# A scan's output store moved to two thirds of the next period, with a third output buffer (hybrid decoder trunk, one core)

## The chip, the core and the metric

The kernel runs on one core of a Trainium2 chip. Five engines work beside each other and meet through semaphores: PE (matrix products; PEld loads the stationary operand), DVE and ACT (elementwise work, also out of PSUM), POOL (elementwise work in SBUF) and SP, which here only issues transfers. Each engine takes its instructions in the order in which the program has them. The metric is device microseconds of one execution, the median of three runs.

## The reference, cut to what matters

Two layers run over 1024 tokens of width 1024: first a convolution and gating mixer, then RWKV-7 time mixing, each followed by a gated feed-forward network, with layer norms between. The change touches the recurrence of the second layer, with 16 heads of width 64:

```python
def step(state, inp):
    r_t, w_t, k_t, v_t, kk_t, a_t = inp
    sa = jnp.einsum('bhij,bhj->bhi', state, -kk_t)
    state = (state * w_t[:, :, None, :]
             + sa[..., None] * (kk_t * a_t)[:, :, None, :]
             + v_t[..., None] * k_t[:, :, None, :])
    return state, jnp.einsum('bhij,bhj->bhi', state, r_t)
_, y = lax.scan(step, state0, ...)
...
y = ((y - ym) * lax.rsqrt(yv + GN_EPS)).reshape(bsz, s, d) * ln_g + ln_b
y = y + bonus.reshape(bsz, s, d)
return ((y * g) @ w_out).astype(x.dtype)
```

## The kernel before, in words

The phases run one after another: `phase_a` (first mixer), `ffn`, `phase_c` (projections of the second mixer, spilled to DRAM), `phase_d` (the recurrence, "the scan"), `phase_e` (output projection) and `ffn` again. `phase_d` is a generator, which `phase_c` drives for its first steps and `phase_e` for the rest, with products of their own traced between its steps.

The scan cuts the 1024 positions into 16 chunks of 64 and the heads into two groups of 8. That makes 32 **units**, each a chunk of one group, in the order chunk by chunk. One turn of the loop at L1438 is a **period**. In period i several units are worked on at different stages, each a generator: `cumulate` (E in the order string; unit i+4), `decay` (D; unit i+3), `scores` (P; unit i+2), `inverse` (I; unit i+1) and `chain` (C; unit i). The string `ORDER` of 28 letters says which generator takes its next step. The order is that of tracing; a scheduler then sets each engine's own order from its model of durations and from the dependencies, so an operation may end up some periods ahead of where it was traced. A dependency made by `pace` only tells this scheduler to place an instruction behind the last product traced; on the chip nothing waits for it.

What matters here, with the lines of the profile:

- **Loads, all issued by SP**: `load` fetches the logarithmic decays SW and the keys KN (L1195, one tile `ld` for both), the keys K and KA (L1199, four transfers) and R (L1201). `load_v` fetches the values twice, into `UV` (L1211, a tile named `ra`) and into `V` (L1212, a tile named `R`), two transfers each. The names of tiles in a profile are those of the big tile from which a ring of small buffers was cut, so `R` stands for many things and the line tells them apart.
- **`cumulate`**: DVE's running sum over SW (L1218), then L1221; ACT's exponentials of it (L1224, L1226, L1228).
- **`decay`**: ACT L1238 and L1239, DVE L1243, L1246, L1247, POOL L1249.
- **`inverse`**: five levels of small products (pX, pQ), each with an ACT copy (L1304) and two DVE copies (L1313, L1317).
- **`chain`**: products with the state, ACT copies (L1345, L1351, L1356, L1366), the state's update (DVE L1375, POOL L1376), then statistics of the output on DVE (L1386, L1387), ACT L1389, and a run of POOL operations on the output y: L1391, L1395, L1396, L1397, L1400 and L1407, where y is done. POOL's L1399 prepares `bo`, the bonus that L1400 adds; it reads `V`, and there are three buffers of `V` and two of `bo`.
- **`store`** (L1418): two transfers of y to DRAM (L1422), traced at the start of the next period, ahead of that period's loads.

So one instruction stream on SP carries 13 transfers for each unit: 2 stores and 11 loads. `phase_e` reads y back in rows of 128 tokens (L174 from `scr_y`), loads the weights `w_o` (L174) through three `wraw` buffers, and splits them on ACT (L189) and DVE (L190); some of that is traced into the last periods of the scan.

Of the kernel before, what the change touches and what calls it, by code (L numbers as in the profile page):

```python
# [72 lines left out]
AHEAD = 4  # L73
INV = 1

ORDER = "ICIPCEIPDICPIECDICPICICPDICI"
SCAN_EARLY = 32


# [77 lines left out]
def small(c, shape, name, tag, bufs=4):  # L157
    return c.pool.tile(shape, F32, name=name, tag=tag, bufs=bufs)


def bank(c, which, name, shape=None, dtype=F32):
    return c.psum.tile(shape or [P, 512], dtype, name=name, tag="ps" + which,
                       bufs=dict(a=NB_A, b=NB_B, c=NB_C)[which])
# [39 lines left out]
def pace(c, ins):  # L203

    return after(c, ins, c.last_mm)


def after(c, ins, dep):

    c.tc.add_manual_dep(ins.ins, dep.ins.name, mybir.DependencyInfo(  # L210
        mybir.DependencyClass.NoSync, mybir.DependencyReason.SCHED_ONLY), reason="pace")
    return ins
# [836 lines left out]
def level_view(ap, m, second):  # L1049

    v = ap.rearrange("p h (b e m) -> p h b e m", e=2, m=m)
    return v[:, :, :, 1 if second else 0, :]
# [71 lines left out]
def phase_d(c, scr, scrv, scry, l_g2):  # L1124
# [10 lines left out]
    nc, tc, sc = c.nc, c.tc, c.scan  # L1135
    NG = NH // 2 // HP
# [5 lines left out]
    half = [slice(0, 64), slice(64, 128)]  # L1142
# [3 lines left out]
    def rings(plan, n, dtype=F32):  # L1146
        pool, at = Ring(c, plan[0][0], n, sum(k for _, k in plan), dtype).bufs, 0
        for name, k in plan:
            r = Ring.__new__(Ring)
            r.bufs, r.i = pool[at:at + k], 0  # L1150
            at += k
            R1[name] = r
    rings([("ra", INV + 3), ("bk", 2), ("bktm", NA), ("UV", INV + 3), ("AT", 2 * NA)], 2 * W)
    rings([("R", 3), ("cl", 2), ("Em", 2), ("rk", 2), ("S", 2 * NG), ("dS", 2), ("u1", 2), ("y", 2),
           ("V", 3), ("gg", 2), ("bo", 2)], W)
    rings([("E", 4)], HP * (CH + 2))
    rings([("TT", 2)], HP * P, F32R)
# [4 lines left out]
    for i, t_ in enumerate(R1["AT"].bufs):  # L1162
        e = 1 - i % 2
# [5 lines left out]
    S = [None] * NG  # L1169
# [9 lines left out]
    def mm(*a, **k):  # L1179
        keep(nc.tensor.matmul(*a, **k))  # L1180

    def tr(*a):
        keep(nc.tensor.transpose(*a))

    def load(n, ch, g):
        u = Ctx()
        u.n, u.ch, u.g = n, ch, g
        ks = slice(g * HP, (g + 1) * HP)
        at = slice(ch % 2 * CH, ch % 2 * CH + CH)
        src = lambda nm, r=slice(0, P): scr[nm][ch // 2, r, ks, at]  # L1190
        u.ld = {}
        t_ = tmp(c, "ld")
        for e, nm in enumerate(("SW", "KN")):
            u.ld[nm] = A4(t_[:, e * W:(e + 1) * W])
            nc.sync.dma_start(u.ld[nm], src(nm))  # L1195
        u.xk = tmp(c, "ld").rearrange("p (k x t) -> p k x t", k=HP, x=2)
        for e in range(2):
            for x, nm in ((e, "K"), (1 - e, "KA")):
                nc.sync.dma_start(u.xk[half[e], :, x, :], src(nm, half[e]))  # L1199
        u.ld["R"] = A4(R1["R"]())  # L1200
        nc.sync.dma_start(u.ld["R"], src("R"))  # L1201
        us[n] = u

    def load_v(u):

        src = scrv[u.ch * CH:(u.ch + 1) * CH, u.g * 2 * W:(u.g + 1) * 2 * W].rearrange(
            "t (k e j) -> t e k j", k=HP, e=2)
        u.UV = R1["UV"]().rearrange("p (e k j) -> p e k j", e=2, k=HP)
        u.V = A4(R1["V"]())
        for e in range(2):  # L1210
            nc.sync.dma_start(u.UV[half[e], e], src[:, e])  # L1211
            nc.sync.dma_start(u.V[half[e]], src[:, e])  # L1212
# [21 lines left out]
    def decay(u):  # L1234

        ld = u.ld
        E, Em = u.clx, A4(R1["Em"]())
        nc.scalar.activation(Em, E[:, :, 1:CH + 1], AF.Exp, scale=CDEC)  # L1238
        nc.scalar.activation(E[:, :, 1:CH + 1], E[:, :, 1:CH + 1], AF.Exp, scale=-CDEC)  # L1239
        u.ra = A4(R1["ra"]())  # L1240
        u.bk, u.rk = A4(R1["bk"]()), A4(R1["rk"]())
        yield
        nc.vector.tensor_tensor(u.bk.rearrange("p k (x t) -> p k x t", x=2), u.xk,  # L1243
                                Em.unsqueeze(2).to_broadcast([P, HP, 2, CH]), op=ALU.mult)
        yield
        nc.vector.tensor_tensor(u.ra[:, :, 0:CH], ld["R"], E[:, :, 1:CH + 1], op=ALU.mult)  # L1246
        nc.vector.tensor_tensor(u.ra[:, :, CH:], ld["KN"], E[:, :, 0:CH], op=ALU.mult)  # L1247
        for e in range(2):
            nc.gpsimd.tensor_tensor(u.rk[half[e]], ld["R"][half[e]], u.xk[half[e], :, e, :], op=ALU.mult)  # L1249
        yield  # L1250

    def scores(u):
        u.AT = [A4(R1["AT"]()) for _ in range(2)]
        u.lt = A4(R1["lt"]())

        ps = [bank(c, "c", "pA", [P, HP, P]) for _ in range(2)]
        for k, e in PAIRS:
            mm(ps[e][:, k, :], u.bk[half[e], k, :], u.ra[half[e], k, :], start=True, stop=True)
            if (k, e) == (HP // 2 - 1, 1):
                yield  # L1260
        for e in range(2):
            nc.vector.copy_predicated(u.AT[e], sc.mA.rearrange("p k x t -> p k (x t)"), ps[e])
            o = half[1 - e]
            nc.scalar.copy(u.lt[o, :, o], u.AT[e][o, :, CH:])
        yield

        pb = bank(c, "c", "pb")
        for k, e in PAIRS:
            mm(pb[half[e], k:k + 1], u.rk[half[e], k, :], c.colr("r_k", u.g * HP + k, 1)[half[e]],
               start=True, stop=True)  # L1270
        u.bon = small(c, [P, HP], "bon", "bon", NA)
        nc.vector.tensor_copy(u.bon, pb[:, 0:HP])
        yield

        p = bank(c, "c", "ptm", [P, HP, P])
        for k in range(HP):
            tr(p[:, k, :], u.bk[:, k, :], c.ident)
        u.bktm = A4(R1["bktm"]())
        nc.scalar.copy(u.bktm, p)
        u.Tm, u.Tt = A4(R1["Tm"]()), A4(R1["Tt"]())  # L1280
        idb = sc.ident16.unsqueeze(1).to_broadcast([P, HP, P])
        nc.scalar.copy(u.Tm, idb)
        nc.scalar.copy(u.Tt, idb)
        yield
        u.L = A4(R1["L"]())
        p16 = bank(c, "b", "pL", [P, HP, P], F16)
        for k in range(HP):
            tr(p16[:, k, :], u.lt[:, k, :], sc.ident16)
        nc.scalar.copy(u.L, p16)
        nc.vector.copy_predicated(level_view(u.Tt, 1, True), sc.mTT[1].unsqueeze(3), level_view(u.lt, 1, True))  # L1290
        nc.vector.copy_predicated(level_view(u.Tm, 1, False), sc.mT[1].unsqueeze(3), level_view(u.L, 1, False))
        yield
# [118 lines left out]
    seq = [(ch, g) for ch in range(T // CH) for g in range(NG)]  # L1411
    us = {}

    def through(gen):
        for _ in gen:
            pass

    def store(u):  # L1418
        dst = scry[u.ch * CH:(u.ch + 1) * CH, u.g * 2 * W:(u.g + 1) * 2 * W].rearrange(
            "t (k e j) -> t e k j", k=HP, e=2)  # L1420
        for e in range(2):
            nc.sync.dma_start(dst[:, e], u.y[half[e]])  # L1422

    def by_half(name):

# [11 lines left out]
    through(decay(us[0]))  # L1437
    for i in range(-INV - 1, len(seq)):  # L1438
        gens = {}
        if i > 0:  # L1440
            store(us[i - 1])
        if i + AHEAD + 1 < len(seq):
            load(i + AHEAD + 1, *seq[i + AHEAD + 1])
        if 0 <= i + INV + 1 < len(seq):
            load_v(us[i + INV + 1])
        if i + AHEAD < len(seq):
            gens["E"] = cumulate(us[i + AHEAD])
        if i + INV + 2 < len(seq):
            gens["D"] = decay(us[i + INV + 2])
        if i >= 0:  # L1450
            gens["C"] = chain(us[i], us.get(i + NG))
        if 0 <= i + INV < len(seq):
            gens["I"] = inverse(us[i + INV])
        if i + INV + 1 < len(seq):
            gens["P"] = scores(us[i + INV + 1])
        if i == 0:
            g2 = c.pool.tile([P, 1024], F32, name="g2", tag="w", bufs=N_W)
            nc.sync.dma_start(g2, l_g2)
            g2 = g2.rearrange("p (g k e j) -> p g e k j", g=NG, k=HP, e=2)
            lg, lb = by_half("rln_g"), by_half("rln_b")  # L1460
        for s in ORDER:
            if s in gens:
                fresh[0] = True
                next(gens[s], None)
                if s in "CIP":
                    yield
        for gen in gens.values():
            assert next(gen, "end") == "end"
    store(us[len(seq) - 1])

def phase_e(c, scry, xres, w_o, scan, res):
# [52 lines left out]
    def through(gen):  # L1527
        for _ in gen:
            pass
    total = 32 * sum(ORDER.count(s) for s in "CIP") - SCAN_EARLY  # L1530
    rows_ = [big(c, "g_row"), c.pool.tile([P, 1024], F32, name="b_row", tag="w", bufs=N_W)]
# [112 lines left out]
```

## Time and profile before

| | us |
|---|---|
| median of three runs (2683.39, 2683.41, 2695.26) | 2683.41 |
| the profiled execution | 2686.94 |
| its span, first to last instruction | 2685.1 |
| SP's wait for L1407 or L1399 at L1422, 1420 to 1862 us | 172.5 |
| DVE's wait for SW at L1218, same stretch | 24.3 |

The page gives busy time by engine and in 40 slices. The views used below are the windows (busy time of each engine in a stretch, and the granted clock), the waits (who waited for whom, in total) and the timelines of single engines, where a bracket behind a row is the idle time before it and what ended it. A wait for several semaphores is put down to the one that came last.

### The profile page before, as it was taken

To read this page: it belongs to the slowest core of one execution; us is meant where nothing else is said; L and a number is where in the kernel's file an instruction comes from. 1 tells how busy PE (TensorE), PEld (TensorE's weight loads), DVE (VectorE), ACT (ScalarE), POOL (GpSimd) and SP (SyncE) were. 2 spreads that over 40 slices of the span, in tenths; PEclk is the share of its full clock that TensorE was granted. 3 is DMA by queue.
4 is the path that set the end of the run, shared out by engine and by line. 5 is a ranking of instruction groups with operands and counts; after the bars stand their busy time and mean duration, and the time that the engine had idled before them with its cause. 6 is when DMAs were issued, how large, how long until landed. Compare 5 with 4: busy or idle time off the path is not lost. (4 is left out here: it accounts for less than half of the span.)

```text
span 2685.1 us, 41451 instructions
## 1 busy us (share of the span) xinstructions
PE 2533.1 (94%) x16064; PEld 2018.1 (75%) x16064; DVE 1672.4 (62%) x2981; ACT 1135.9 (42%) x2192; POOL 505.3 (19%) x526
## 2 busy tenths in 40 slices
PE   8999989999989999999998888888899999998998
PEld 7677867888868787777777767776778888876776
DVE  7675596666645427777846767675387666644435
ACT  3116542333324217777746666574252333323320
POOL 0012250000041000010214555456200000023003
PEclk9999999999999998999998889799899999998999
DMA  3403322222245322555764343323122222235531
GB/s 143 124 25 114 107 85 88 86 77 81 79 160 199 135 99 95 168 153 177 203 165 101 92 95 88 69 48 131 67 102 102 79 79 86 79 130 183 177 106 63
DMA packets 258181, 297.89 MB, mean 111 GB/s; under 512 B 149952, under 2 KB 191040, under 8 KB 257984
## 3 DMA queue, kind: packets, MB, share of 16 engines
q1 hardware_dynamic: 256832, 293.14, 34.4%
q8 instruction: 126, 2.06, 0.3%
q10 hardware_dynamic: 1152, 2.10, 0.2%
q14 instruction: 71, 0.58, 0.1%
HBM read 221.66 MB, written 69.21 MB: 108 GB/s over the span
## 5 line engine op out<-in xcount | busy, mean ns | idle before, releaser
L641 PE MATMUL py<-xch,wb 128*128 128x512 f32 x1056 | 356.6, 400 | 4.4 <-DVE u L690 2.4
L229 PE MATMUL pd<-wb,hh 128*128 128x512 f32 x704 | 282.2, 401 | 21.9 <-ACT wb L197 14.2
L197 ACT CAST wb<-wraw 128x512 fp32r<-128x512 f32 x220 | 135.2, 619 | 376.8 <-PE py L641 173.9
L231 PE MATMUL pd<-wb,hl 128*128 128x512 f32 x704 | 281.9, 400 | 6.9 <-DVE hl L200 6.9
L230 PE MATMUL pd<-wb,hh 128*128 128x512 f32 x704 | 281.4, 400 | 1.5 <-DVE wb L200 1.5
L200 DVE TENSOR_TENSOR wb<-wraw,wb 128x512 fp32r<-128x512 f32 x220 | 161.0, 735 | 145.1 <-ACT wb L197 143.0
L641 PEld LDWEIGHTS py<-xch,wb 128*128 128x128 f32 x1056 | 200.3, 190 | 62.8 <-DVE u L690 15.7
L641 PE MATMUL pz<-xch,wb 128*128 128x512 f32 x704 | 233.4, 393 | 4.5 <-ACT xch L197 4.5
L641 PE MATMUL px<-xch,wb 128*128 128x512 f32 x704 | 233.9, 395 | 3.2 <-ACT p L652 3.2
L352 POOL TENSOR_TENSOR acc<-acc,g_row 128x1024 f32<-128x1024 f32 x24 | 62.4, 2605 | 845.3 <-DMA acc<-res 824.0
L197 ACT CAST wb<-sums 128x512 fp32r<-128x512 f32 x176 | 108.6, 621 | 257.1 <-PE pz L641 144.3
L641 PE MATMUL py<-xcl,wb 128*128 128x512 f32 x528 | 209.4, 397 | 1.6 <-DVE xcl L200 1.6
L200 DVE TENSOR_TENSOR wb<-sums,wb 128x512 fp32r<-128x512 f32 x176 | 123.2, 703 | 102.3 <-ACT wb L197 101.5
L200 DVE TENSOR_TENSOR hl<-wraw,hh 128x1024 fp32r<-128x1024 f32 x76 | 107.1, 1411 | 115.8 <-ACT hh L197 115.8
L229 PEld LDWEIGHTS pd<-wb,hh 128*128 128x128 f32 x704 | 135.7, 193 | 55.7 <-ACT wb L197 15.5
L231 PEld LDWEIGHTS pd<-wb,hl 128*128 128x128 f32 x704 | 135.0, 192 | 38.2 <-DVE hl L200 7.8
L1180 PEld LDWEIGHTS <-lt 128*128 128x128 f16 x1792 | 88.5, 103 | 97.1 <-issue 71.3
L230 PEld LDWEIGHTS pd<-wb,hh 128*128 128x128 f32 x704 | 135.2, 192 | 33.4 <-DVE wb L200 2.7
L641 PEld LDWEIGHTS pz<-xch,wb 128*128 128x128 f32 x704 | 132.5, 189 | 34.5 <-ACT xch L197 5.3
L641 PEld LDWEIGHTS px<-xch,wb 128*128 128x128 f32 x704 | 131.9, 188 | 34.9 <-ACT p L652 5.5
L269 POOL TENSOR_TENSOR rstd<-ve,mhalf 128x1 f32<-128x1 f32 x48 | 37.9, 792 | 627.0 <-DVE ve L267 590.9
L1180 PE MATMUL pX<-lt 128*128 128x64 f16 x1280 | 92.3, 201 | 63.1 <-DVE lt L1313 33.4
(311 smaller groups left out, 5779.4 us busy)
## 6 DMA issues: line engine op xcount, KB each, us to landing
wraw<-in_f_in_dram SPq DMA_DIRECT2D x96, 512.0 KB, 3.6
wraw<-scr_h SPq DMA_DIRECT2D x76, 512.0 KB, 3.9
scr_h<-hf SPq DMA_DIRECT2D x44, 512.0 KB, 2.6
wraw<-in_f_out_dram SPq DMA_DIRECT2D x88, 256.0 KB, 3.0
res<-acc SPq DMA_DIRECT2D x16, 512.0 KB, 2.6
acc<-res SPq DMA_DIRECT2D x16, 512.0 KB, 6.7
wraw<-in_w_r_dram SPq DMA_DIRECT2D x16, 512.0 KB, 3.8
wraw<-in_w_k_dram SPq DMA_DIRECT2D x16, 512.0 KB, 4.2
```

Of the source, the lines that this page charges most:

```text
L197: nc.scalar.copy(hi, src)
L200: return (eng or nc.vector).tensor_tensor(lo, src, f(hi), op=ALU.subtract)
L229: nc.tensor.matmul(ps, ls(ah), rs(bh), start=start, stop=False)
L230: nc.tensor.matmul(ps, ls(ah), rs(bl), start=False, stop=False)
L231: c.last_mm = nc.tensor.matmul(ps, ls(al), rs(bh), start=False, stop=stop)
L269: c.last_pow = nc.gpsimd.tensor_tensor(r, ve, c.mhalf[:, 0:1], op=ALU.pow)
L352: c.nc.gpsimd.tensor_tensor(x, x, rows[0], op=ALU.mult)
L641: c.last_mm = nc.tensor.matmul(ps, a_[:, k * P:(k + 1) * P], b_[:, k % 2, :], start=start and k == i == 0, stop=False, skip_group_check=True)
L1180: keep(nc.tensor.matmul(*a, **k))
```

## The change

`store` becomes a generator with one step, its two transfers carry a `pace`, and a letter Y in `ORDER`, the 21st of now 29 letters, says where that step is taken. It still stores the unit of the period before. The ring of y buffers grows from two to three; the rings of that plan take 27 in place of 26 quarter tiles, and seven big tiles hold 28.

```diff
-ORDER = "ICIPCEIPDICPIECDICPICICPDICI"
+ORDER = "ICIPCEIPDICPIECDICPIYCICPDICI"
...
-    rings([("R", 3), ("cl", 2), ("Em", 2), ("rk", 2), ("S", 2 * NG), ("dS", 2), ("u1", 2), ("y", 2),
+    rings([("R", 3), ("cl", 2), ("Em", 2), ("rk", 2), ("S", 2 * NG), ("dS", 2), ("u1", 2), ("y", 3),
...
         for e in range(2):
-            nc.sync.dma_start(dst[:, e], u.y[half[e]])
+            pace(c, nc.sync.dma_start(dst[:, e], u.y[half[e]]))
+        yield
...
-        if i > 0:
-            store(us[i - 1])
         if i + AHEAD + 1 < len(seq):
             load(i + AHEAD + 1, *seq[i + AHEAD + 1])
...
             gens["P"] = scores(us[i + INV + 1])
+        if i > 0:
+            gens["Y"] = store(us[i - 1])
...
-    store(us[len(seq) - 1])
+    through(store(us[len(seq) - 1]))
```

The scheduler's order changes on SP, ACT, DVE and POOL and not on PE. Three places follow. A number in a name is a buffer, and a bracket names the semaphores that an instruction waits for: `Pool_49` counts POOL's instructions, `DMAHWn_49` earlier transfers.

**SP, in the middle of the scan.** Before, the store of unit 14 stood ahead of `V` of unit 19 (L1212) and of SW of unit 23:

```order
L1422 DMA scr_y_81<-R_10298 64x4x64 [waits DMAHW5_49,Pool_49]
L1422 DMA scr_y_81<-R_10298 64x4x64 [waits DMAHW6_49]
L1212 DMA R_10299<-scr_v_80 64x4x64 [waits DMAHW7_49,Pool_49]
L1212 DMA R_10299<-scr_v_80 64x4x64 [waits DMAHW0_49]
L1195 DMA ld_13762<-scr_SW_79 128x4x64 [waits DMAHW1_49,DVE_49]
```

In some periods the next unit's SW stood ahead of the store, as here SW of unit 24 and the store of unit 15:

```order
L1195 DMA ld_14008<-scr_SW_79 128x4x64 [waits DMAHW2_49,DVE_49]
L1422 DMA scr_y_81<-R_10298 64x4x64 [waits DMAHW3_49,Pool_49]
L1422 DMA scr_y_81<-R_10298 64x4x64 [waits DMAHW4_49]
L1212 DMA R_10299<-scr_v_80 64x4x64 [waits DMAHW5_49,Pool_49]
L1212 DMA R_10299<-scr_v_80 64x4x64 [waits DMAHW6_49]
```

Now every period has this order, here with `V` of unit 19, SW of unit 23 and the store of unit 14:

```order
L1212 DMA R_10299<-scr_v_80 64x4x64 [waits DMAHW6_49,Pool_49]
L1212 DMA R_10299<-scr_v_80 64x4x64 [waits DMAHW7_49]
L1195 DMA ld_13760<-scr_SW_79 128x4x64 [waits DMAHW0_49,DVE_49]
L1195 DMA ld_13760<-scr_KN_77 128x4x64 [waits DMAHW1_49]
L1201 DMA R_10294<-scr_R_75 128x4x64 [waits DMAHW2_49,DVE_49,Pool_49]
L1422 DMA scr_y_81<-R_10298 64x4x64 [waits DMAHW3_49]
L1422 DMA scr_y_81<-R_10298 64x4x64 [waits DMAHW4_49]
```

The store has moved behind SW, KN and (mostly) R, and has lost its wait for POOL; the first of the two `V` loads keeps one, and now stands ahead of SW in every period. In both programs the counts say that `V` of unit n waits for L1399 of unit n-3, which stands on POOL directly behind L1407 of unit n-5, the output that the store of unit n-5 takes.

**DVE, around L1218 of unit 20** (the profile names this operation TENSOR_TENSOR_SCAN). Before:

```order
L1313 COPY_PREDICATED lt<-mk_1_3128,pX 128x32x8
L1317 COPY_PREDICATED lt<-mk_0_3122,pQ 128x32x8
L1243 TENSOR_TENSOR ra<-ld,R 128x512
L1218 SCALAR_TENSOR_TENSOR R<-rst,ld 128x256
L1375 TENSOR_TENSOR R<-pS,R 128x256
```

Now:

```order
L1313 COPY_PREDICATED lt<-mk_1_3128,pX 128x32x8
L1317 COPY_PREDICATED lt<-mk_0_3122,pQ 128x32x8
L1218 SCALAR_TENSOR_TENSOR R<-rst,ld 128x256
L1243 TENSOR_TENSOR ra<-ld,R 128x512
L1375 TENSOR_TENSOR R<-pS,R 128x256
```

In 15 of the 22 units from 10 to 31 L1218 now stands ahead of L1243 and L1375, and in the other 7 between the two. ACT's L1238, which needs L1243, stands behind L1224 in the 15 units, and ahead of it in the 7. Before, L1218 stood at varying places: where SW was ahead of the store it stood up to six rows earlier, ahead of L1246.

**SP, at the end of the scan.** Before, a `w_o` load stood behind the store of unit 29:

```order
L174 DMA wraw_18532<-in_w_o_dram 128x1024 [waits DMAHW4_49,DMAHW1_49,DVE_49]
L1422 DMA scr_y_81<-R_10298 64x4x64 [waits DMAHW5_49,Pool_49]
L1422 DMA scr_y_81<-R_10298 64x4x64 [waits DMAHW6_49]
L174 DMA wraw_18538<-in_w_o_dram 128x1024 [waits DMAHW7_49,DMAHW3_49,DVE_49]
L174 DMA wraw_18544<-scr_y_81 128x1024 [waits DMAHW4_49,DMAHW0_49,DVE_49]
L1494 DMA acc_18548<-xres_74 128x1024
L174 DMA wraw_18594<-scr_y_81 128x1024 [waits DMAHW7_49,DMAHW2_49,DVE_49]
```

Now:

```order
L174 DMA wraw_18532<-in_w_o_dram 128x1024 [waits DMAHW4_49,DMAHW1_49,DVE_49]
L174 DMA wraw_18538<-in_w_o_dram 128x1024 [waits DMAHW5_49,DMAHW3_49,DVE_49]
L174 DMA wraw_18544<-scr_y_81 128x1024 [waits DMAHW6_49,DMAHW4_49,DVE_49]
L1495 DMA acc_18548<-xres_74 128x1024 [waits DMAHW7_49]
L174 DMA wraw_18594<-scr_y_81 128x1024 [waits DMAHW5_49,DMAHW0_49,DVE_49]
L1422 DMA scr_y_81<-R_10298 64x4x64 [waits Pool_49]
L1422 DMA scr_y_81<-R_10298 64x4x64 [waits DMAHW2_49]
```

The last `w_o` load of the scan, two rows of y, and a load of the residual have moved ahead of that store. The `w_o` load's own wait for DVE is for the L190 that frees its `wraw` buffer, the second of the five at the end of the scan.

## Rows read from the trace of the kernel before

**Rows 1.** Page: the span.
```profile
span 2685.1 us, 41451 instructions
```
**Rows 2.** Windows: stretch, length, busy by engine, clock, DMA share, GB/s.
```profile
1440.41:1757.55 317.14, 267.85 (x4494) 229.45 (x4493) 221.82 (x643) 204.04 (x599) 170.84 (x223) 0.85 0.37 87
1650.33:1662.44 12.11, 10.80 (x208) 9.19 (x204) 9.62 (x29) 9.09 (x27) 7.37 (x10) 1.00 0.33 73
1739.89:1754.82 14.93, 14.27 (x209) 12.43 (x206) 10.04 (x29) 9.59 (x29) 5.48 (x8) 0.66 0.29 64
```
**Rows 3.** Waits, 1420 to 1862: total us, times, longest.
```profile
DVE R L1218 <- DMA ld<-scr_SW: 24.3, 12, 3.8
...
SPq L1422 <- POOL R L1399: 145.2, 28, 11.1
SPq L1422 <- POOL R L1407: 27.3, 3, 13.0
```
**Rows 4.** Timeline of POOL: unit 11's y, then unit 12's.
```profile
1583.08 0.73 POOL L1407 TENSOR_TENSOR R<-R 128x256 f32<-128x256 f32 x1
1583.77 0.61 POOL L1399 TENSOR_TENSOR R<-R,bon 128x256 f32<-128x256 f32 x1
...
1597.97 0.72 POOL L1407 TENSOR_TENSOR R<-R 128x256 f32<-128x256 f32 x1
```
**Rows 5.** Timeline of SP's issues in the same stretch.
```profile
1583.84 1.25 SPq L1422 DMA_DIRECT2D scr_y<-R  x2
1585.19 1.25 SPq L1212 DMA_DIRECT2D R<-scr_v  x2
1586.54 0.55 SPq L1195 DMA_DIRECT2D ld<-scr_SW  x1
```
**Rows 6.** Timeline of DVE in the same stretch.
```profile
1586.13 0.69 DVE L1243 TENSOR_TENSOR ra<-ld,R 128x512 f32<-128x512 f32 x1
1589.72 0.69 DVE L1218 TENSOR_TENSOR_SCAN R<-rst,ld 128x256 f32<-128x256 f32 x1 [2.90 <-DMA ld<-scr_SW]
```
**Rows 7.** Timeline of PE in the same stretch.
```profile
1591.12 0.28 PE L1180 MATMUL pX<-lt 128*128 128x64 f16 x4 [2.57 <-DVE lt L1313]
```
**Rows 8.** Timeline of SP, then of DVE, around the store of unit 16.
```profile
1648.37 0.36 SPq L1195 DMA_DIRECT2D ld<-scr_SW  x1
1652.74 1.25 SPq L1422 DMA_DIRECT2D scr_y<-R  x2
...
1653.48 1.21 DVE L1218 TENSOR_TENSOR_SCAN R<-rst,ld 128x256 f32<-128x256 f32 x1
```
**Rows 9.** DMA view, 1440 to 1757: KB each, median us to landing.
```profile
ld<-scr_SW SPq DMA_DIRECT2D x22, 128.0 KB, 2.5
```
**Rows 10.** Timeline of SP, then of DVE: the slowest SW that was waited for.
```profile
1628.03 0.55 SPq L1195 DMA_DIRECT2D ld<-scr_SW  x1
...
1632.63 0.69 DVE L1218 TENSOR_TENSOR_SCAN R<-rst,ld 128x256 f32<-128x256 f32 x1 [1.42 <-DMA ld<-scr_SW]
```
**Rows 11.** A window, and the gap of PE ahead of it.
```profile
1733.00:1750.50 17.50, 17.10 (x210) 14.65 (x211) 11.05 (x37) 9.76 (x30) 7.53 (x11) 0.51 0.29 65
...
1732.94 0.28 PE L1180 MATMUL pX<-lt 128*128 128x64 f16 x4 [3.22 <-DVE lt L1313]
```
**Rows 12.** Timelines of SP, DVE, ACT and PE at the scan's end, and its window.
```profile
1837.84 1.25 SPq L1422 DMA_DIRECT2D scr_y<-R  x2
1839.19 0.54 SPq L174 DMA_DIRECT2D wraw<-in_w_o_dram  x1
...
1829.62 1.22 DVE L190 TENSOR_TENSOR wlo<-wraw,whi 128x1024 fp32r<-128x1024 f32 x1 [2.02 <-ACT whi L189]
...
1843.33 1.04 ACT L189 CAST whi<-wraw 128x1024 fp32r<-128x1024 f32 x1 [9.68 <-DMA wraw<-in_w_o_dram]
...
1844.97 0.37 PE L1180 MATMUL pX<-lt 128*128 128x64 f16 x4 [6.06 <-ACT lt L1304]
...
1842.00:1849.50 7.50, 4.53 (x24) 3.57 (x24) 1.89 (x3) 2.40 (x6) 3.48 (x2) 0.54 0.75 279
```

## The prediction

> **What bounds the kernel now.** The profiled execution took 2686.94 us, its span 2685.1 [rows 1], 3.5 above the median of 2683.41; the sum below is made against 2686.94 and 3.5 are taken off at the end. I read the windows of the scan first. From the store of unit 1 to that of unit 23 are 317.14 us, 22 periods of 14.42 on average. A period without a stall takes 12.11 us at clock 1.00 and 14.93 at a granted clock of 0.66, with PE busy for 10.80 and 14.27 of it [rows 2]. So PE and the chain behind it set a period of about 12 us at 2.4 GHz, and the missing 2.3 us are stalls and stretches at 1.2 GHz. The mean clock of 0.85 says that about 30% of the time is at the lower level (1 - 0.3 x 0.5).
>
> The waits come next. SP waits 172.5 us at the store, 145.2 and 27.3 in two rows, and DVE waits 24.3 us for SW in 12 units [rows 3]. SP's large number costs nothing by itself; what costs is what stands behind it. The timelines of unit 11 show how: POOL ends y (L1407) at 1583.81 [rows 4]; SP, which had waited for that, issues the store at 1583.84, `V` at 1585.19 and SW only at 1586.54 [rows 5]; DVE is through with L1243 at 1586.82, and L1218 starts at 1589.72, having waited 2.90 [rows 6]; PE has a gap of 2.57 [rows 7]. Where SW stood ahead of the store there is none of this: SW issued at 1648.37, the store at 1652.74, and L1218 starts at 1653.48 without a wait [rows 8].
>
> **The scan: the store.** The change takes the store's two issues from ahead of `V` and SW to behind SW and KN. Taken alone, that frees SW from POOL's L1407. But `V` keeps its wait for POOL, which is for L1399, the instruction behind the same L1407, and the order now has `V` ahead of SW in every period. So I expect the wait to move from the store to `V`: SP stands at L1212 where it stood at L1422, and SW, KN and R stand behind it as before. What is won is the store's own time in that queue, 1.35 us (1583.84 to 1585.19, [rows 5]); what is lost is L1399, which ends 0.57 after L1407 (1583.77 + 0.61 against 1583.81, [rows 4]). The net gain is 0.78 us in a unit that stalls today. Against it stand the 10 units of 22 that don't stall today, in which SW would now stand behind the wait too.
>
> **The period that follows.** The stalled unit is a loop from one L1407 to the next. (1) L1407 to `V`: 0.57 + 0.03 for the issue = 0.60. (2) `V`'s pair to SW: 1.35 [rows 5]. (3) SW's issue to L1218: the median landing is 2.5 [rows 9]; unit 11 had 3.18 (1589.72 - 1586.54, [rows 5, 6]); the slowest had 4.60 [rows 10]. I take 2.8, between the median and unit 11, because the store's transfers are no longer just ahead of it; the ends are 2.5 and 4.6. (4) L1218 to the next end of L1407: 8.97 (1589.72 to 1598.69, [rows 4, 6]). These make 13.72. In 15 of the 22 units L1243, and with it ACT's L1238, now stand behind the waiting L1218, where in unit 11 they were done before it. That adds nothing if the chain has slack there, and L1243's 0.69 [rows 6] and a hand-over of about 0.2 (my estimate) if it has none. I take 0.85, near the upper end, since L1375, which carries the chain on, stands behind L1243 on DVE; the ends are 0 and 0.9. So 7 units of 13.72 and 15 of 14.57 make a mean of 14.30, at 2.4 GHz.
>
> **The clock.** A stall in every period makes a gap of PE in every period. After the gap of 3.22 that ended at 1732.94 the clock was 0.51 for 17.5 us [rows 11]. A low period of the old kernel took 14.93 [rows 2]; the loop hides part of that, as (1) to (3) don't depend on PE, and I give a low period 15.2 in place of 14.30. Today 30% of the time is low with 12 stalls; with a stall in each period I take 40%. That is 0.4 x 0.9 = 0.36, and a period of 14.66 against 14.42: 22 x 0.24 = **+5.3**. The ends of (3) and (4) move it widely: landing at the median is -0.3 a period, 22 x 0.3 = 6.6 lower; unit 11's 3.18 in place of 2.8 is 8.4 higher; L1243 at no cost is 15 x 0.85 = 12.8 lower. The slowest landing in every period would be 22 x 1.8 = 40 higher, which one row out of 22 doesn't make likely.
>
> A rule on step (3): the page DMA: Bandwidth & Descriptors of the Trainium skill, section Anatomy of one DMA — SWDGE (gpsimd) path, gives a transfer a fixed 2.0 us and its bytes at 436 GB/s; for 128 KB that is 2.3 us, an estimate from that page. The trace disagrees upward, with 2.5 as the median and 3.18 and 4.60 where DVE waited [rows 5, 6, 9, 10], and the page states it for POOL's path while these are issued by SP. By the page the sum would be 0.5 x 22 = 11 us lower.
>
> **The end of the scan.** Here the change does take a transfer out from behind the wait. The store of unit 29 went out at 1837.84 and the `w_o` load behind it at 1839.19, though that load's buffer was free when L190 ended at 1830.84; ACT got it at 1843.33 after a wait of 9.68, and PE had a gap of 6.06, followed by 7.5 us at clock 0.54 [rows 12]. Now the load stands ahead of that store, issues at about 1831 and lands by 1835 (the same 4.14 us), some 1.4 us after ACT falls idle (1843.33 - 9.68 = 1833.65). The gap goes, -6.06, and some of the slow clock, where PE was busy for 4.53 of 7.50: half of that at the lower level would be given back, about 2. With 1 us for what is late next (DVE's L190 behind ACT's L189) I take **-7**; the ends are -4 (the load still meets `V` loads ahead of it) and -9.
>
> **Edits at nothing.** The `pace` is no wait on the chip. The third y buffer takes the 27th of 28 quarter tiles, so no other ring shrinks; a y is stored about half a period later than before, and the third buffer gives it a whole period more. The loads of y for `phase_e` stand behind later stores, but those of the last units stay behind the same L1407. PE's order doesn't change. If the store's 2 x 0.6 us on SP were to stand where SW is due, the cost would be 1.35 a period, but it stands behind SW.
>
> **Sum.** 2686.94 + 5.3 - 7 = 2685.2; less 3.5 makes a forecast of **2682**.
>
> **Rival A, faster: no wait takes the store's place.** If POOL has done L1399 by the time SP comes to `V`, SW lands before DVE needs it in all units, as in the units with SW ahead of the store [rows 8]. The period would be 12.11 with a few at the low clock, 12.3: 22 x (14.42 - 12.3) = 47 less, and 7 at the end: 2683 - 54 = 2629. Half of that, where `V` is late in every other unit, gives 2656. Against it: in the timeline L1399 ends 0.57 us behind the very instruction for which SP waits today [rows 4], and SP has no more to do ahead of it than before. Chance 0.17.
>
> **Rival B, slower: the clock stays low through the scan.** Place: PE's gap in each period behind L1218. If each gap of 2 us or so is followed by a low stretch as long as a period, as at 1733 to 1750.5 [rows 11], all periods are low ones, of 14.93 and what the loop doesn't hide, 15.4 by my estimate: 22 x 0.98 = 21.6 more, less 7: 2698. It decides, against my bound of 13.4, from a period of 14.42 + (13.4 + 7)/22 = 15.35, or from SW landing 0.7 later than I took it. For it: nearly every unit gets a gap; against it: in the loop at low clock PE fills its own gap, since a PE that needs 14.27 of 14.93 [rows 2] has none. The page TensorE: Matmul & The Clock Gate of the Trainium skill, section A second HAM failure mode: psum-queue depth-cycling, says that short idling of PE between groups, often repeated, makes the clock swing between its two levels. By that rule this rival comes true; the trace agrees as far as one gap of 3.22 and the 0.51 behind it go. Chance 0.26.
>
> **The forecast's own case** is that the change doesn't do what it says: the store moves and the wait stays. Chance 0.57, with a range of its own of 2670 to 2697.
>
> **How the numbers follow.** Within 0.5% (13.4 us, about what a measurement of this kernel can tell from no change) lies 2670 to 2697. The range that leaves out 2 in 10 cuts off rival A beyond its mildest third and the upper third of rival B, where slow landings add to a low clock: 2664 to 2704.
>
> **What would show it.** Right: SP's wait for L1399 stands at L1212 and none at L1422; L1218 waits for SW in about 22 units, 35 to 50 us in all; the mean period is 14.2 to 15.2; ACT's wait of 9.68 and PE's gap of 6.06 at the end are gone. Wrong towards A: L1218 waits for SW seldom, and a period is below 13. Wrong towards B: the clock over the same 22 periods is below 0.75. Wrong in the tail: the `w_o` load still lands after 1840.

## The result, and the profile after

The changed kernel is slower: 2703.60 us against 2684.85 (medians of 11 runs each); the ratio of the means is 1.0058, with an interval of 1.0041 to 1.0075. The forecast was 2682, which could not be told from no change; the time lies in the stated range, but as a loss, on the side of rival B. The profiled execution took 2705.01, its span is 18.2 us longer than that of [rows 1]:

```profile
span 2703.3 us, 41451 instructions
```

Where the 18.2 went follows from the ends of L1407 of units 1 and 23, 22 periods apart (in the kernel before at 1440.38 and 1757.52, [rows 2] to within 0.03). The 22 periods took 341.51 in place of 317.14: **+24.4**. From there to the end are 919.9 us (2703.3 - 1783.41) in place of 927.6: **-7.7**. Ahead of unit 1 is +1.5.

The windows of the kernel after; the columns are those of [rows 2]. The first row is the 22 periods, the next two are the periods of units 16 and 17, and the last two are stretches cut where the clock changes:

```profile
1441.90:1783.41 341.51, 296.22 (x4486) 254.08 (x4485) 216.05 (x642) 204.03 (x599) 169.22 (x223) 0.74 0.36 80
1660.10:1674.38 14.28, 11.53 (x160) 9.64 (x161) 7.66 (x27) 8.41 (x25) 7.38 (x12) 0.74 0.34 76
1674.38:1691.02 16.64, 15.84 (x252) 13.92 (x251) 11.24 (x33) 9.80 (x31) 7.25 (x12) 0.71 0.31 66
...
1667.00:1684.50 17.50, 16.70 (x206) 14.34 (x204) 10.18 (x36) 9.94 (x30) 7.23 (x10) 0.51 0.30 66
1684.50:1697.50 13.00, 10.41 (x204) 9.01 (x200) 8.43 (x23) 8.01 (x25) 7.17 (x10) 1.00 0.36 78
```

Two kinds of period take turns here, 14.28 and 16.64 (the next two are 14.12 and 16.63). This holds for the last ten of the 22; the twelve ahead of them have no such order and take 13.5 to 18.9. Over the pair the clock is at 1.2 GHz for 17.5 us and at 2.4 for the rest. The mean period is 15.52 and the mean clock 0.74, where it was 14.42 and 0.85.

The waits of DVE, SP and ACT, 1420 to 1880 us (total, times, longest), which answer to [rows 3]:

```profile
DVE R L1218 <- DMA ld<-scr_SW: 29.3, 15, 3.3
...
ACT whi L189 <- DMA wraw<-in_w_o_dram: 3.8, 2, 2.4
...
SPq L1212 <- POOL R L1399: 134.8, 27, 7.4
...
SPq L1422 <- POOL R L1399: 17.7, 2, 11.1
```

The wait has moved from the store (145.2) to `V` (134.8), as forecast; the waits left at the store are those at the end of the scan. The timelines of POOL, SP, DVE and PE over that pair of periods answer to [rows 4 to 7]:

```profile
1659.37 0.73 POOL L1407 TENSOR_TENSOR R<-R 128x256 f32<-128x256 f32 x1
1673.65 0.73 POOL L1407 TENSOR_TENSOR R<-R 128x256 f32<-128x256 f32 x1
1690.29 0.73 POOL L1407 TENSOR_TENSOR R<-R 128x256 f32<-128x256 f32 x1
...
1660.70 1.24 SPq L1212 DMA_DIRECT2D R<-scr_v  x2
1662.04 0.55 SPq L1195 DMA_DIRECT2D ld<-scr_SW  x1
...
1674.98 1.24 SPq L1212 DMA_DIRECT2D R<-scr_v  x2
1676.31 0.55 SPq L1195 DMA_DIRECT2D ld<-scr_SW  x1
...
1664.60 0.69 DVE L1218 TENSOR_TENSOR_SCAN R<-rst,ld 128x256 f32<-128x256 f32 x1 [2.11 <-DMA ld<-scr_SW]
1675.14 1.34 DVE L1262 COPY_PREDICATED ra<-mA,pA 128x512 f32<-128x512 uint8 x2 [2.91 <-PE pA L1180]
1679.62 0.68 DVE L1218 TENSOR_TENSOR_SCAN R<-rst,ld 128x256 f32<-128x256 f32 x1
...
1666.59 0.28 PE L1180 MATMUL pX<-lt 128*128 128x64 f16 x4 [1.76 <-DVE lt L1313]
```

The reader sees the loop as the prediction built it. L1407 ends at 1660.10, `V` goes out 0.60 later, SW 1.34 after that, and L1218 starts at 1664.60 with a wait of 2.11; PE has a gap of 1.76, and 0.4 us later, at 1667, the clock falls. In the following period SP does the same at the same distances, but DVE itself is late: with the clock at 1.2 GHz it has waited 2.91 for PE at L1262. L1218 starts 3.31 after SW's issue, without a wait, and L1407 ends 11.40 after it in place of 9.78. So there is no gap in that period, the clock rises at 1684.5, and the next period stalls again.

### The profile page after: what moved, and what is told of

Same layout as the page of the kernel before. It is cut to its first block, busy times and chain, and to the rows that moved or that the text cites. A ratio compares the mean times of both kernels' runs of the same rounds, so it can differ in the third digit from the quotient of the medians.

```text
span 2703.3 us, 41451 instructions
## 1 busy us (share of the span) xinstructions
PE 2558.4 (95%) x16064; PEld 2038.9 (75%) x16064; DVE 1670.6 (62%) x2981; ACT 1136.7 (42%) x2192; POOL 504.5 (19%) x526
## 4 chain that ended last, share of the span: by engine, by line
PE 67%; issue 10%; DVE 8%; DMA 6%; ACT 5%; POOL 4%; SPq 0%; DVEq 0%; POOLq 0%; ACTq 0%
PE py L641 13%; PE pz L641 8%; PE px L641 8%; DMA wraw<-scr_h 2%; PE pA L1180 2%; PE pX L1180 2%; PE pv L229 2%; PE po L229 1%; PE po L230 1%; PE pv L230 1%; PE po L231 1%; PE pv L231 1%; PE pd L229 1%; PE pd L230 1%; PE pd L231 1%
## 5 line engine op out<-in xcount | busy, mean ns | idle before, releaser
L200 DVE TENSOR_TENSOR wb<-wraw,wb 128x512 fp32r<-128x512 f32 x220 | 160.9, 735 | 147.7 <-ACT wb L197 145.2
L229 PEld LDWEIGHTS pd<-wb,hh 128*128 128x128 f32 x704 | 134.8, 192 | 57.8 <-ACT wb L197 18.7
L1180 PE MATMUL pX<-lt 128*128 128x64 f16 x1280 | 98.2, 209 | 58.6 <-DVE lt L1313 34.5
```

Source lines behind the costliest of these rows:

```text
L200: return (eng or nc.vector).tensor_tensor(lo, src, f(hi), op=ALU.subtract)
L229: nc.tensor.matmul(ps, ls(ah), rs(bh), start=start, stop=False)
```

## The experiments

All edits are to the changed kernel or to the one before, as each says. Ratios are to the kernel before.

**V behind the store.** In `load_v` only the first three units load V; the others do so in `store`:

```diff
         for e in range(2):
             pace(c, nc.sync.dma_start(dst[:, e], u.y[half[e]]))
+        if u.n + 3 < len(seq):
+            w = us[u.n + 3]
...
+            for e in range(2):
+                pace(c, nc.sync.dma_start(w.V[half[e]], src[:, e]))
         yield
```

> The change, with the loads into V (L1212) taken from load_v and traced behind the store, for the unit three later; V then waits for an L1399 that ended a period earlier, and SW has no transfer ahead of it that waits for POOL. Theory 1 (V's wait for L1399 stands ahead of SW on SP and makes the stall): L1218 no longer waits for SW in the scan, the clock of the 22 periods rises from 0.74 to above 0.95, the period falls from 15.5 to 12.1 to 12.6 us, and the time to 2625 to 2645 us. Rival 2 (the new order on DVE and ACT, with L1218 ahead of L1243 and L1375, is what costs): that order stays, so the time stays at 2695 to 2710 us.

Measured: 2639.18 us, ratio 0.9827 [0.9812, 0.9841], the fastest kernel of this study. Windows of it, 21 periods and then one:

```profile
1458.69:1712.54 253.85, 221.76 (x4284) 192.72 (x4284) 193.60 (x610) 189.40 (x568) 155.63 (x212) 1.00 0.43 95
...
1615.39:1627.48 12.09, 10.56 (x204) 9.18 (x204) 9.17 (x31) 9.00 (x27) 7.39 (x12) 1.00 0.44 96
```

The period is 12.09 at clock 1.00, and of the waits for SW one of 0.35 is left in these periods. L1218 still stands ahead of L1243 and L1375 on DVE there (L1219, L1244 and L1376 in this kernel), so that order costs nothing by itself: rival 2 falls.

```profile
1617.71 0.68 DVE L1219 TENSOR_TENSOR_SCAN R<-rst,ld 128x256 f32<-128x256 f32 x1
1618.31 0.66 DVE L1244 TENSOR_TENSOR ra<-ld,R 128x512 f32<-128x512 f32 x1
1618.89 0.41 DVE L1376 TENSOR_TENSOR R<-pS,R 128x256 f32<-128x256 f32 x1
```

**Four buffers of V** in the changed kernel:

```diff
-            ("V", 3), ("gg", 2), ("bo", 2)], W)
+            ("V", 4), ("gg", 2), ("bo", 2)], W)
```

> The change with four buffers of V in place of three; nothing else is edited, V waits for the L1399 of a unit earlier. Theory 1: the wait is over when SP comes to it, as in the run with V behind the store: period 12.1 to 12.8 us, clock above 0.93, time 2625 to 2650 us. Rival 2 (order on DVE and ACT): 2695 to 2710 us. Rival 3 (V's wait is not the releaser, SW waits for its own buffer, freed by DVE's L1247): L1218 still waits for SW, 2690 to 2710 us.

Measured: 2644.80 us, 0.9845 [0.9831, 0.9860]. `V` still waits for POOL, but for an L1399 one unit earlier, and no wait for SW is left, so rival 3 falls too. `V` and the store both stand ahead of SW here (the scheduler has moved SW behind the store), and SP waits 66.0 us at `V` (1450 to 1780); the waits end before SW is due. So it is not SP's wait as such that costs. It is 22 periods of 12.82 at clock 0.96:

```profile
SPq L1212 <- POOL R L1399: 66.0, 24, 7.4
...
1451.54:1733.56 282.02, 244.66 (x4502) 209.55 (x4503) 222.89 (x644) 203.64 (x598) 175.16 (x223) 0.96 0.42 96
```

**Four buffers of V in the kernel before**, the same edit there. The scheduler then puts the store, with its wait for POOL, ahead of SW in more periods than before, though not in every one as was expected: in 17 of the 21 of the window below, against 14 of 22 in the kernel before.

> The kernel before with four buffers of V and nothing else: the store stays where it was traced, keeps its wait for L1407, and now stands ahead of SW in every period, not in about half of them; V stands behind SW. Theory 1 (any wait for POOL's y ahead of SW in every period costs, no matter which transfer carries it): as slow as the change in the scan, period 15.0 to 15.8 us, clock 0.70 to 0.80, and without the change's gain at the end of the scan: 2695 to 2720 us. Rival 2, that the move of the store itself costs: no slower than before, 2678 to 2692 us.

Measured: 2701.66 us, 1.0062 [1.0047, 1.0077], as slow as the change without any of it. The waits of DVE and SP, and a window of 21 periods, 15.28 each:

```profile
DVE R L1218 <- DMA ld<-scr_SW: 26.3, 14, 3.7
...
SPq L1422 <- POOL R L1399: 157.0, 29, 11.1
```

```profile
1451.61:1772.53 320.92, 279.12 (x4290) 239.27 (x4289) 207.71 (x615) 195.22 (x572) 161.89 (x214) 0.76 0.35 83
```

So the same loss comes with the wait on the store as with the wait on `V`. What goes with the loss is in how many periods SW stands directly behind such a wait: 14 of 22 before, 17 of 21 here, all 22 in the change. In the two fast kernels what stands ahead of SW has its wait for POOL over before SW is due.

**Two buffers of y** in the changed kernel, `("y", 2)`.

> The change with two buffers of y, as before: the move of the store alone. Theory 1: the third buffer plays no part, V's wait stays ahead of SW: 2695 to 2712 us, period 15.3 to 15.8 us. Rival 4 (the third buffer lets POOL run ahead and shifts L1399): back to 2680 to 2690 us; and if the store frees y too late with two buffers, DVE's L1394 would wait for the store, and it would be slower than 2715 us.

Measured: 2700.22 us, 1.0049 [1.0029, 1.0068]: the loss is there without the third buffer.

**The third buffer alone**, `("y", 3)` in the kernel before, and **the end alone**: the same, and from unit 24 on the store is taken at Y. The edit of the end is shown against the changed kernel:

```diff
+        if 0 < i < 25:
+            through(store(us[i - 1], False))
...
+        if i >= 25:
+            gens["Y"] = store(us[i - 1])
```

> The kernel before with three buffers of y and nothing else. Theory 1: no order of SP in the scan's middle changes, within 3 us of the kernel before. Rival 4 (the third buffer by itself matters): over 8 us away.

> The kernel before, with three buffers of y and the store moved only from unit 24 on; up to there it is traced as before. Theory on the end of the scan (a w_o load behind the store of unit 29 made PE wait 6.06 us): that gap goes and the scan's first 22 periods stay at 14.4 us: 6 to 8 us faster than before. Rival 6 (the gap at the end is only moved, ACT or DVE being next): within 2 us of the kernel before. To be compared with the run of the third buffer alone.

Measured: 2692.25, 1.0023 [1.0007, 1.0040], and 2685.37, 0.9998 [0.9983, 1.0013]. The end alone is 6.9 us faster than the third buffer alone, as expected; in the two profiles the stretch from L1407 of unit 23 on is 9.0 shorter (919.6 and 928.6), and the 22 periods ahead of it are 3.3 longer. But the third buffer alone came out 6 us slower than before, which was not expected: its edit also moves some hundred instructions on DVE. Which of them cost is left open; the profiled execution, at 2686.26 one of the fastest of that kernel, doesn't show the loss. The end of the scan with the third buffer alone, ACT and PE:

```profile
1841.60 1.04 ACT L189 CAST whi<-wraw 128x1024 fp32r<-128x1024 f32 x1 [8.97 <-DMA wraw<-in_w_o_dram]
...
1843.24 0.37 PE L1180 MATMUL pX<-lt 128*128 128x64 f16 x4 [4.19 <-ACT lt L1304]
```

With the end alone, PE has no such gap and ACT waits 0.94:

```profile
1838.85 1.05 ACT L189 CAST whi<-wraw 128x1024 fp32r<-128x1024 f32 x1 [0.94 <-DMA wraw<-in_w_o_dram]
```

**One unit.** The kernel with V behind the store, with unit 18 loaded in `load_v`:

```diff
-            if u.n < 3:
+            if u.n < 3 or u.n == 18:
...
-        if u.n + 3 < len(seq):
+        if u.n + 3 < len(seq) and u.n + 3 != 18:
```

> The run with V behind the store (2639 us, period 12.09 at clock 1.00), but for one unit, 18, V is traced in load_v again, so that its wait for L1399 stands ahead of SW of unit 22 once. Theory 1 with the clock: L1218 of unit 22 waits 2 to 3.5 us once, PE gets one gap of over 2 us, the clock falls to 1.2 GHz for up to 17.5 us and comes back by itself; the two periods cost together about 6.6 us (14.3 and 16.5 against 12.1): about 2646 us. Rival 5, that the stall costs only its own length and the low clock of the change comes from something else: one period of about 14.3, the clock stays at 1.00, 2641 us. Rival 2: nothing to be seen.

Measured: 2640.61 us, 0.9833 [0.9810, 0.9856]. DVE (L1219 is L1218 there), PE and the window of that period:

```profile
1600.40 0.69 DVE L1219 TENSOR_TENSOR_SCAN R<-rst,ld 128x256 f32<-128x256 f32 x1 [1.65 <-DMA ld<-scr_SW]
...
1601.46 0.28 PE L1180 MATMUL pX<-lt 128*128 128x64 f16 x4 [1.76 <-DVE lt L1314]
```

```profile
1594.96:1608.93 13.97, 10.96 (x210) 9.41 (x209) 9.65 (x32) 9.43 (x28) 7.49 (x12) 1.00 0.41 89
```

One wait costs 1.9 us (13.97 - 12.09), and here the clock stays at 1.00. The expectation for the clock was wrong: the gap of 1.76 is as long as the one in the change at 1666.59, behind which the clock fell. It is not quite the change's stall, though: in this unit the scheduler has put L1218 behind L1243 and L1375 (L1244 and L1376 there), which the wait therefore doesn't hold up.

```profile
1598.33 0.42 DVE L1376 TENSOR_TENSOR R<-pS,R 128x256 f32<-128x256 f32 x1 [0.34 <-PE pS L1180]
```

**Ten units**, 14 to 23, in place of one (`14 <= u.n < 24`).

> The run with V behind the store, but for units 14 to 23, whose V is traced in load_v again, so that ten periods in a row, which come at full clock, have V's wait ahead of SW. The run with one such unit had a wait of 1.65 us, a gap of PE of 1.76, a period of 13.97 and no low clock. Theory 7, that the turns of high and low clock start by themselves once every period has its gap: within three of the ten periods the clock falls, then periods of about 14.3 and 16.5 in turn; 25 to 35 us longer than 2640. Rival 8, that gaps of this size leave the clock alone and the change's low clock comes from larger ones at the scan's start, which never ends: ten periods of 13.8 to 14.3 at clock 1.00, 15 to 22 us longer than 2640.

Measured: 2649.62 us in one run, 10 more than with none (2639.18). Windows of it: six periods, the one behind them, three more, and a stretch of low clock:

```profile
1577.29:1657.52 80.23, 65.65 (x1178) 56.27 (x1178) 56.96 (x173) 54.16 (x163) 44.94 (x61) 0.94 0.39 87
1657.52:1674.55 17.03, 16.10 (x256) 14.15 (x253) 11.47 (x33) 10.11 (x31) 7.45 (x11) 0.70 0.37 79
1674.55:1711.94 37.39, 32.50 (x618) 27.60 (x616) 29.93 (x89) 27.43 (x82) 23.04 (x31) 1.00 0.38 80
1650.50:1668.00 17.50, 16.41 (x206) 14.47 (x204) 9.91 (x33) 9.95 (x30) 7.23 (x10) 0.51 0.30 65
```

The figures of both theories missed, and the run doesn't try what it was meant to. `V` of units 14 to 23 goes ahead of SW of units 18 to 27, and of these only five wait for SW, 0.8 to 2.1 us. L1218 stands on DVE as in the change only for units 25 to 27; for 23 it is behind L1243 and L1375, for 24 between them. Units 26 and 27 then make the change's pair: a wait of 2.09 in a period of 14.26, the clock at 0.51 for 17.5 us, and a period of 17.03 without a wait. There the edit ends: the last `V` ahead of SW goes out at 1658.11, and in the three periods of 12.46 that follow, SW goes out 3 to 5 us ahead of L1218.

```profile
1647.73 0.69 DVE L1219 TENSOR_TENSOR_SCAN R<-rst,ld 128x256 f32<-128x256 f32 x1 [2.09 <-DMA ld<-scr_SW]
...
1658.11 1.23 SPq L1213 DMA_DIRECT2D R<-scr_v  x2
1659.44 0.55 SPq L1195 DMA_DIRECT2D ld<-scr_SW  x1
```

So whether the turns would have kept on stays open here.

**Products at the gap, first try.** In the changed kernel, nine products of 128x128 by 512 in each period:

```diff
+            if m == 16:
+                for _ in range(FILL):
+                    mm(pX.rearrange("p a k t -> p (a k t)"), L[:, 0, :], flat(L), start=True, stop=True)
```

> The change, with nine more products of 128x128 by 512 (2.0 to 2.5 us at 2.4 GHz, a result that is overwritten) in each period, ahead of the products of the fourth of the five levels of inverse, where PE waits for DVE behind L1218. Theory with the clock: L1218 still waits for SW, PE works through its gap and the clock stays near 1.00 (above 0.93 against 0.74), so the low period of 16.5 us goes and all are 14.0 to 14.8 us: 2670 to 2690 us, faster than the change though it computes more. Rival 5 (the low clock doesn't come from the gap): the products only add work, some 2 us in the low periods: 2715 us or more.

Measured: 2681.57 us, 0.9985 [0.9970, 1.0000], the time that was expected but not for the reason. The scheduler moved L1218 and L1399 too, DVE waits for SW only twice (3.0 us), and so nothing follows on the clock.

**Products at the gap, the order kept.** The products stand at `m == CH // 2`, and `after`, which only ties the scheduler, holds L1218 behind the copy L1317 that it follows in the change, and L1399 behind the L1407 that it follows. With no products in them, these ties give the changed kernel's order on DVE, ACT, POOL and SP.

```diff
+        if n - 7 in l8:
+            after(c, ins, l8[n - 7])
...
+        if u.n - 2 in l7:
+            after(c, ins, l7[u.n - 2])
```

> The change with ten products of 128x128 by 512 (about 2.4 us at 2.4 GHz by the 245 ns of one in the run before; their result is overwritten) ahead of the products of the fifth level of inverse, where PE waits behind L1218; L1218 and L1399 are tied to the places that they have in the change, so that V's wait stays ahead of SW and behind the same L1407, and the DVE order around L1218 stays. Theory with the clock: L1218 waits for SW in most units as before, but PE works through the wait, the clock of the 22 periods rises from 0.74 to above 0.93, and all periods take 13.8 to 14.8 us in place of 14.3 and 16.5 in turn: 2665 to 2690 us. Rival 5 (the gap isn't what lowers the clock): clock near 0.74, low periods of 17.5 to 19 us, 2715 to 2740 us.

> The same with five products (1.2 us). Theory with the clock: half of each gap is filled; if a gap of about 1 us is harmless, the clock is above 0.90 and the time 2660 to 2690 us; if any gap lowers the clock, it stays below 0.80 and the time is 2695 to 2715 us. Rival 5: 2705 to 2725 us.

Measured: with ten products 2705.48 us, 1.0065 [1.0043, 1.0088]; with five 2694.03 us, 1.0026 [1.0013, 1.0038]. Here the times mislead and the windows tell. Twenty periods, of units 4 to 23, in the change, then with ten products and with five:

```profile
1472.38:1783.41 311.03, 269.23 (x4080) 230.85 (x4080) 195.44 (x584) 185.20 (x544) 153.80 (x203) 0.74 0.35 80
```

```profile
1475.05:1766.62 291.57, 258.75 (x4282) 204.14 (x4284) 187.03 (x581) 186.31 (x541) 147.04 (x202) 0.99 0.36 80
```

```profile
1472.56:1764.38 291.82, 242.90 (x4168) 198.05 (x4166) 190.82 (x580) 184.19 (x541) 150.12 (x203) 0.96 0.36 81
```

The wait for SW is still there, in 20 and in 21 units (L1221 is L1218 in both kernels):

```profile
DVE R L1221 <- DMA ld<-scr_SW: 26.4, 20, 2.6
```

```profile
DVE R L1221 <- DMA ld<-scr_SW: 35.6, 21, 2.8
```

The clock stays at 0.99 and 0.96, most low periods go, and the twenty periods take 14.58 and 14.59 us each in place of 15.55, though they hold ten or five more products each. So the wait and the low clock come apart: at much the same wait for SW (29.3 us in the change) the low clock is worth about 19 us of these periods (311.03 - 291.6), nearly all that they lose against the kernel before, where they took 290.13.

What was expected of the gap did not come about. PE doesn't work through it: the products wait for the same copy of DVE, L1313 (L1321 in these kernels), and run behind the gap. Gaps of over 1 us are left in 9 of the twenty periods with ten products and in 14 with five. With five, a product behind a gap of 2.33, and the window of its period:

```profile
1657.16 1.36 PE L1181 MATMUL pX<-lt 128*128 128x512 f16 x9 [2.33 <-DVE lt L1321]
...
1649.32:1664.65 15.33, 11.79 (x215) 9.70 (x211) 9.37 (x30) 9.20 (x28) 7.24 (x11) 1.00 0.33 71
```

This gap is longer than the change's 1.76, and the clock stays at 1.00, in the next period too; behind shorter ones of the same run, of 1.57 and 1.92, it fell for about 3 us. So the length of the gap doesn't decide alone. That more work of PE behind it keeps the clock up is shown; what it is in PE's work around the gap that decides is not.

What was expected of the whole time was wrong as well. With ten products the time ahead of these periods is 2.7 us longer, that from unit 23 to the end of the scan 9.1 (four periods without a wait take 13.1 us each in place of 12.0), and the stretch behind the scan, which holds none of these products, 8.9; the cause of the last is open.

## Why the prediction was wrong

**The store's wait moves to V, and SW stays behind it.** Right. The wait is at L1212, and the kernels without it ahead of SW are the fast ones.

**The stalled period.** Right in its length: 14.30 was forecast for the loop at full clock, 14.28 and 14.12 were measured. These periods are not at full clock, though (0.74 in both). It seems to cost nothing in them, as a stalled period of the run with ten units, which is at 1.00, has the same (4): 1643.26 - 1633.47 = 9.79.

```profile
1633.47 0.69 DVE L1219 TENSOR_TENSOR_SCAN R<-rst,ld 128x256 f32<-128x256 f32 x1 [0.96 <-DMA ld<-scr_SW]
...
1629.07:1643.26 14.19, 11.52 (x232) 10.05 (x229) 10.36 (x33) 9.89 (x30) 7.23 (x11) 1.00 0.47 114
```

The terms: (1) and (2) 1.94 against 1.95; (3) 2.56 against 2.8; (4) 9.78 against 8.97 + 0.85 = 9.82. Over the 15 units that waited, (3) is 2.4 to 3.9 and 2.8 in the mean. For it the page DMA: Bandwidth & Descriptors of the Trainium skill, section Anatomy of one DMA — SWDGE (gpsimd) path, gave an estimate of 2.3; all 15 are above that.

**The clock.** Here is the step that failed. "I give a low period 15.2 in place of 14.30", and 40% of them. Measured: 16.64 in the pair above, and every second one. Over all 22, the eleven with a wait of more than 1 us take 14.85 in the mean and the other eleven 16.19, which makes the 15.52; the forecast's period was 14.66. That is +24.4 in place of +5.3, and with the end and the stretch ahead of unit 1 the 18.2 of the profiles.

The 15.2 was built on the 14.93 of [rows 2], and that row runs from one L1351 to the next, while the loop (1) to (4) runs from one end of L1407 to the next. Measured like the loop, the same period took 17.00, and the one ahead of it, with the stall of 3.23, took 15.18. So the trace before held the price and the turns already:

```profile
1725.34:1740.52 15.18, 11.34 (x158) 9.38 (x158) 7.83 (x26) 8.00 (x25) 7.37 (x11) 0.76 0.35 79
1740.52:1757.52 17.00, 16.03 (x258) 14.06 (x256) 12.00 (x34) 10.76 (x32) 7.31 (x11) 0.72 0.25 56
```

The other half of the error is the claim that the loop hides the low clock, as (1) to (3) don't depend on PE. But (4) does: it took 11.40 in place of 9.78, and (3) became 3.31, because DVE came late (over the seven periods without a wait (4) is 9.7 to 11.8 and (3) 3.3 to 5.1). A stall in one period and a slow PE in the next add up; they don't overlap.

**Stalls in 22 units, 35 to 50 us.** Wrong: 15 and 29.3, eleven of them over 1 us. In the periods at the low clock DVE is late itself and waits little or not at all.

**The end of the scan.** Right: -7.7 against -7. ACT's longest wait of 9.68 [rows 12] is 2.4, PE's gap of 6.06 is gone. The end alone against the third buffer alone gives 6.9 by the medians and 9.0 by the profiles.

**Rival B** came true in its price (15.4 a period forecast, 15.5 measured) and in its sign (mean clock 0.74, where below 0.75 was named), though not in its manner: not all periods are low, but about every second one, and those are slower than it took. The page TensorE: Matmul & The Clock Gate of the Trainium skill, section A second HAM failure mode: psum-queue depth-cycling, has a clock that swings where PE idles shortly and often. The change shows such a swing, in its last ten periods with 17.5 us at the lower level in each 31; a single gap of 1.76 in an undisturbed scan did not lower the clock, nor did one of 2.33 with five more products behind it. **Rival A** is what the change becomes when V is taken from ahead of SW: 12.09 a period where 12.3 was forecast, 2639 us where 2629 was.

## What to carry to other kernels

When a wait is taken off one transfer of an in-order queue, look at the next transfer in that queue: if it waits for the same work, the load that matters gains nothing, and if the new order puts that load behind it in every period, it loses. What counts is what stands ahead of the load that an engine will need soon; a load that has periods to spare (here V) belongs behind it. And where a short gap of PE recurs, cost it with the low clock that follows: take a stalled period and the slow one behind it as a pair, both between the same two marks.

## What the runs showed of the hardware that was not expected

- In the last ten periods of the change, gaps of PE of 1.6 to 2.9 us in every second one went with a granted clock of 0.51 for 17.5 us in each 31. Five or ten needless products in each period, which run behind the gap, kept the clock of twenty periods at 0.96 and 0.99 in place of 0.74, and made these periods shorter.
- A gap's length does not tell whether the clock falls: it fell behind gaps of 1.59 and 1.76 in the change, and did not behind one of 1.76 in a scan that ran at full clock, nor behind one of 2.33 that had five products behind it.
